# Feed-forward weights of a hybrid encoder block: every low part made by GpSimd, row differences in four parts, down's first activations loaded earlier

## The chip, the cores and the metric

The kernel runs on 1 core of one Trainium2 chip. The metric is the device time of one execution in microseconds (us), given as the median of several runs. A profiled execution is one more run, with a trace of every instruction on the engines: PE (matrix products; PEld is its weight load), DVE (VectorE), ACT (ScalarE), POOL (GpSimd) and SP (SyncE, which here only issues DMAs). Each engine works through its own queue in the order in which the program was laid out, and a waiting instruction holds up all that stands behind it.

## The reference, cut to what matters

All data is float32: x is 1024 rows of 1024, and the change touches only the last part of the layer, the gated feed-forward network of width 2816.

```
hs = hs + mixer_block(rmsnorm(hs, norm_mix), ...)
h  = rmsnorm(hs, norm_ffn)
hs = hs + (silu(h @ w_gate) * (h @ w_up)) @ w_down      # 1024 -> 2816 -> 1024
out = rmsnorm(hs, norm_final)[meta rows dropped]
```

## The kernel before, in words

**Precision.** A float32 product is made of three products of a shorter type (`F32R`): each operand x is cast on ACT to its high part h (`wh`, `yah`, `oph`), and another engine subtracts, l = x - h (`wl`, `yal`, `opl`). I call the first the cast and the second the rest. Every product then runs hh, hl and lh into one PSUM tile.

**Stages.** The mixer ends with `o0` to `o3` (line 1152) at about 1551 us. Then follows the network: 22 keys `wg0`, `wu0`, ... `wg10`, `wu10`, each 256 columns of the gate or up weights, and after them 11 keys `wd0` to `wd10` of the down weights. `gate_up_plain` (line 1169) runs `wg0` and `wu0` as plain products: 8 products of 24 matmuls, in the order half 0 of the rows (two of `wg0`, two of `wu0`), then half 1. The other 20 keys go through `wino` (line 1195): a Strassen-Winograd scheme in which the 2 x 2 blocks of the weights (A11, A12, A21, A22) and of the rows (B11 to B22) are combined, so that seven products of 12 matmuls replace eight. Their order is A11, A12, S2, S3, S1, A22, S4. I call one such key a block.

**Weights.** `next_w` (line 188) keeps one key loaded ahead of the one in use. `load_wino` (line 147) loads a key in two halves on SP (line 157; I call them the first and the second half; A11 and A21 lie in the first, A12 and A22 in the second). POOL makes the sums in place: S1 = A21 + A22 (line 179), A21 = A11 - A21, which is S3 (line 180), A11 = S1 - A11, which is S2 (line 181), and A12 = A12 - A11, which is S4 (line 184). Each of the seven matrices is split in `split_q` (cast line 172, rest line 173). The rests of A11, A12, S2 and S3 go to DVE, those of S1, A22 and S4 to POOL. Two tiles limit the overlap: the raw halves have two buffers (`wraw`), so the first half of the next key waits until S3 and the S4 sum of this key are made, and its second half until the rest of S4 is made; S3, A22 and S4 have three tiles in all (`yah`, `yal`), so they wait for products 4, 6 and 7 of the key before.

**Evacuation.** Six PSUM tiles rotate under the products (`pc`; the names mm, yo, ss, cb, yo, yd). Product 1 is copied out by ACT (line 1214), the others are added up on DVE (`plus`, line 1210, tile `mu`). A gate key's four results go through Silu on ACT (line 1232), an up key's are multiplied on DVE (line 1164, tile `fsg`) and stored by SP (line 1165, `d_act`).

**Rows.** `norm2_second(k)` (line 1110) makes, for one k of 4, the second half of the rows and their differences T1, T2, T3: eight transposes on PE (line 1092, tile `tp`, two buffers), casts on ACT, and seven DVE and three POOL operations (lines 1096 to 1130). All four parts are traced right behind the first of the eight plain products. Behind them the pool of `hs` closes, and the pool `fa` (the tiles fsg, mu, s1, yah, yal) opens in its place, which is what `fa_box` says.

**Down.** `load_act(s)` (line 1236) reads four activation tiles back (line 1244) and splits them (cast line 1245, rest line 1246 on DVE and POOL in turn). `load_act(0)` is traced behind the last block, then eight loads of `hs` (line 1255); `down` (line 1257) runs 16 products of 6 matmuls (line 1266) a key and adds each into `hs` on DVE (line 1268).

**What sets the order.** The code is traced in program order; a planner (the scheduler of the kernel framework) then lays out each engine's queue before the run. It goes by what it reckons to be ready, by its own durations, and takes what was traced earlier among what is ready. So a queue can hold an operation of the next key ahead of one of this key, and on the chip that order is fixed.

Of the kernel before, what the change touches and what calls it, by code (L numbers as in the profile page):

```python
# [8 lines left out]
F32 = mybir.dt.float32  # L9
F32R = mybir.dt.float32r  # L10
AF = mybir.ActivationFunctionType
ALU = mybir.AluOpType
# [3 lines left out]
P = 128  # L16
# [14 lines left out]
NFF = FF // P  # L31
# [26 lines left out]
def tile_hybrid_block(  # L58
# [7 lines left out]
    V, S, GP, PE, SP = nc.vector, nc.scalar, nc.gpsimd, nc.tensor, nc.sync  # L66
    x = x[0]
    out = out[0]
# [55 lines left out]
    plan = []  # L124
    ready = []

    def load_w(view, lo):

        a, b = view.shape[1], view.shape[2]
        wh = wts.tile([P, 2048], F32R, name="wh", tag="wh")  # L130
        wl = wts.tile([P, 2048], F32R, name="wl", tag="wl")
        h3 = wh[:, : a * b].rearrange("p (a b) -> p a b", b=b)
        l3 = wl[:, : a * b].rearrange("p (a b) -> p a b", b=b)
        st = a // 2
        for i in range(2):
            raw = wts.tile([P, 1024], F32, name="wraw", tag="wraw", bufs=2)
            r3 = raw[:, : st * b].rearrange("p (a b) -> p a b", b=b)
            SP.dma_start(out=r3, in_=view[:, i * st:(i + 1) * st, :])
            sl = slice(i * st, (i + 1) * st)
            S.copy(out=h3[:, sl], in_=r3)  # L140
            (V if lo[i] == "v" else GP).tensor_tensor(out=l3[:, sl], in0=r3, in1=h3[:, sl].bitcast(F32), op=ALU.subtract)  # L141
        return h3, l3
# [3 lines left out]
    def load_wino(view):  # L146

        fa = fa_box[0]
        raws = []
        for i in range(2):
            raw = wts.tile([P, 1024], F32, name="wraw", tag="wraw", bufs=2)
            r3 = raw.rearrange("p (a b) -> p a b", b=256)
            SP.dma_start(out=r3, in_=view[:, 4 * i:4 * i + 4, :])
            raws.append(r3)
        a11, a21, a12, a22 = (raws[h][:, :, j * P:(j + 1) * P] for h in range(2) for j in range(2))
        wh = wts.tile([P, 2048], F32R, name="wh", tag="wh")  # L160
        wl = wts.tile([P, 2048], F32R, name="wl", tag="wl")
        slots = [tuple(t[:, 512 * i:512 * i + 512] for t in (wh, wl)) for i in range(4)]
        k4 = lambda t: t.rearrange("p (a b) -> p a b", b=P)
        res = {}

        def split_q(name, src, eng):
            if name in ("S3", "A22", "S4"):
                pair = tuple(fa.tile([P, 512], F32R, name=n_, bufs=3) for n_ in ("yah", "yal"))
            else:
                pair = slots.pop(0)  # L170
            h, l = (k4(t) for t in pair)
            S.copy(out=h, in_=src)  # L172
            eng.tensor_tensor(out=l, in0=src, in1=h.bitcast(F32), op=ALU.subtract)  # L173
            res[name] = h, l

        s1 = k4(fa.tile([P, 512], F32, name="s1", bufs=1))
        split_q("A11", a11, V)
        split_q("A12", a12, V)
        GP.tensor_tensor(out=s1, in0=a21, in1=a22, op=ALU.add)
        GP.tensor_tensor(out=a21, in0=a11, in1=a21, op=ALU.subtract)  # L180
        GP.tensor_tensor(out=a11, in0=s1, in1=a11, op=ALU.subtract)
        split_q("S2", a11, V)
        split_q("S1", s1, GP)
        GP.tensor_tensor(out=a12, in0=a12, in1=a11, op=ALU.subtract)  # L184
        split_q("S3", a21, V)
        split_q("A22", a22, GP)
        split_q("S4", a12, GP)
        return res

    def next_w(key):  # L190

        while plan and len(ready) < 2:
            k, view, lo = plan.pop(0)
            ready.append((k, load_wino(view) if lo is None else load_w(view, lo)))
        k, w = ready.pop(0)
        assert k == key, (k, key)
        return w
# [328 lines left out]
    sgs = []  # L526
# [124 lines left out]
    def op_tile():  # L651
        h = opp_box[0].tile([P, 512], F32R, name="oph", tag="oph")
        l = opp_box[0].tile([P, 512], F32R, name="opl", tag="opl")
        return h, l
# [323 lines left out]
    def halves(hh):  # L978
        return slice(hh * 512, hh * 512 + 512)
# [131 lines left out]
    def norm2_second(k):  # L1111

        ps = norm2_cols(1, k)
        b12 = B["B12", k] = split_cols(ps, k, x_pair("x", 4))
        h11, l11 = (t.bitcast(F32) for t in B["B11", k])
        t1 = fx.tile([P, 512], F32, name="t1", bufs=2)
        V.scalar_tensor_tensor(out=t1, in0=ps, scalar=prm(R_NF, k), in1=h11, op0=ALU.mult, op1=ALU.subtract)
        V.tensor_tensor(out=t1, in0=t1, in1=l11, op=ALU.subtract)
        B["T1", k] = split_t(op_tile(), t1, GP)
        ps = norm2_cols(1, k + 4)  # L1120
        B["B22", k] = split_cols(ps, k + 4, op_tile())
        if k % 2 == 0:
            t2f[0] = fx.tile([P, D], F32, name="t2", bufs=2)
        t2 = t2f[k + 1] = t2f[0][:, 512 * (k % 2):512 * (k % 2) + 512]
        V.scalar_tensor_tensor(out=t2, in0=ps, scalar=prm(R_NF, k + 4), in1=t1, op0=ALU.mult, op1=ALU.subtract)
        B["T2", k] = split_t(x_pair("y", 8), t2, GP)
        t3 = fx.tile([P, 512], F32, name="t3", bufs=2)
        V.scalar_tensor_tensor(out=t3, in0=ps, scalar=prm(R_NF, k + 4), in1=b12[0].bitcast(F32), op0=ALU.mult,
                               op1=ALU.subtract)
        V.tensor_tensor(out=t3, in0=t3, in1=b12[1].bitcast(F32), op=ALU.subtract)  # L1130
        B["T3", k] = split_t(x_pair("y", 8), t3, GP)
# [31 lines left out]
    def act_out(s, j, hh, ps_or_sum, sg):  # L1163
        V.tensor_tensor(out=sg, in0=ps_or_sum, in1=sg, op=ALU.mult)
        SP.dma_start(out=d_act[2 * s + j, :, halves(hh)], in_=sg)
# [2 lines left out]

    def gate_up_plain(s):

        ws, sgs = [next_w(f"wg{s}")], {}
        for hh in range(2):
            for u_ in range(2):
                if u_ == len(ws):
                    ws.append(next_w(f"wu{s}"))
                wh, wl = ws[u_]
                for j in range(2):
                    js = slice(j * P, (j + 1) * P)
                    ps = pc()
                    o = [B[(("B11", "B21"), ("B12", "B22"))[hh][k // 4], k % 4] for k in range(KC)]  # L1180
                    mm3(ps, [wh[:, k, js] for k in range(KC)], [wl[:, k, js] for k in range(KC)],
                        [t[0] for t in o], [t[1] for t in o])
                    if not fa_box:
                        with tc.issue_after(last_mm[0].ins):
                            for k in range(4):
                                norm2_second(k)
                        hs_ctx.close()
                        fa_box.append(fa_ctx.enter_context(tc.tile_pool(name="fa", bufs=1)))
                    if u_ == 0:
                        sgs[j, hh] = fa_box[0].tile([P, 512], F32, name="fsg", bufs=4)  # L1190
                        S.activation(out=sgs[j, hh], in_=ps, func=AF.Silu)
                    else:
                        act_out(s, j, hh, ps, sgs.pop((j, hh)))

    def wino(key, emit):

# [24 lines left out]
        emit(1, 0, plus(prod("A22", "T4"), u3, u3))  # L1221
        emit(0, 1, plus(prod("S4", "B22"), u, u))

    gate_up_plain(0)
    for k in range(4):
        norm2_last(k)
    for s in range(1, NFF // 2):
        sgs = {}

        def emit_gate(j, hh, r):  # L1230
            sgs[j, hh] = fa_box[0].tile([P, 512], F32, name="fsg", bufs=4)
            S.activation(out=sgs[j, hh], in_=r, func=AF.Silu)

        wino(f"wg{s}", emit_gate)
        wino(f"wu{s}", lambda j, hh, r: act_out(s, j, hh, r, sgs.pop((j, hh))))


    def load_act(s):

        res = {}  # L1240
        for hh in range(2):
            for j in range(2):
                h, l = res[j, hh] = op_tile()
                SP.dma_start(out=l.bitcast(F32), in_=d_act[2 * s + j, :, halves(hh)])
                S.copy(out=h, in_=l.bitcast(F32))
                (V, GP)[j].tensor_tensor(out=l, in0=l.bitcast(F32), in1=h.bitcast(F32), op=ALU.subtract)
        return res

    res = load_act(0)
    fa_ctx.close()  # L1250
    fx_ctx.close()
    ffp = ctx.enter_context(tc.tile_pool(name="ffp", bufs=2))
    hs = [ffp.tile([P, D], F32, name=f"hs{i}", bufs=1) for i in range(NTT)]
    for i in range(NTT):
        SP.dma_start(out=hs[i], in_=d_hs[i])

    def down(s, res, after=None):
        wh, wl = next_w(f"wd{s}")
# [45 lines left out]
                q.dma_start(out=out[i * P:(i + 1) * P, t0:t0 + n], in_=h_)  # L1304

    for s in range(NFF // 2):
        nxt = load_act(s + 1) if s + 1 < NFF // 2 else None
        down(s, res, None if nxt else final_norm)
        res = nxt

# [28 lines left out]
```

## Time and profile before

| | us |
|---|---|
| median of 3 runs (2266.1 to 2270.68) | 2270.66 |
| profiled execution, its own time | 2271.47 |
| its span, first to last instruction | 2269.8 |
| busy in the span: PE / DVE / POOL / ACT | 2174.4 / 1525.8 / 1060.0 / 824.8 |
| mean granted TensorE clock | 0.995 of full speed |

A row of the timeline is: start, duration, engine, line, operation, out<-in, count, and in square brackets the time that the engine stood idle before it and what ended that. Busy times of PE include the modelled ends of pipelined matmuls, so two neighbours overlap; the spacing of starts is the safer measure.

### The profile page before, as it was taken

The numbers are of one execution on the slowest core, as the hardware profiler recorded it, in microseconds if no ns is written. First come the engines' busy times: TensorE is split into PE (matmuls) and PEld (weight loads), VectorE is DVE, ScalarE is ACT, GpSimd is POOL, SyncE is SP. The second block draws the span as 40 slices with busy tenths as digits, with TensorE's granted clock in tenths as the row PEclk, the third lists the DMA queues.
The fourth block names the chain that finished last, engine by engine and source line by source line (L and its number), as shares of the span: only waits on it lengthen the run. The fifth ranks groups of instructions, "written<-read, shape, count | busy, mean of one in ns | idle before, by whom it ended". The sixth has DMA issues, their size and how long they took to land.

```text
span 2269.8 us, 31785 instructions
## 1 busy us (share of the span) xinstructions
PE 2174.4 (96%) x11863; PEld 1854.1 (82%) x11863; DVE 1525.8 (67%) x1932; ACT 824.8 (36%) x1522; POOL 1060.0 (47%) x887
## 2 busy tenths in 40 slices
PE   7999999999999999988899999998999999989998
PEld 7999999999998766665676778897888777768886
DVE  4389898997881487877897665527544544467666
ACT  6333342323232355444555554214322222231212
POOL 3383755822112486867787331015554445443212
PEclk9999999999999999999999999999999999999999
DMA  4222222233236575756763742412222222263211
GB/s 141 80 67 83 75 75 75 75 119 106 85 110 201 179 220 164 213 156 202 228 184 113 264 149 94 143 60 92 72 75 75 81 77 70 89 250 102 95 64 75
DMA packets 238147, 276.83 MB, mean 122 GB/s; under 512 B 20776, under 2 KB 176024, under 8 KB 237992
## 3 DMA queue, kind: packets, MB, share of 16 engines
q1 hardware_dynamic: 225176, 253.35, 35.8%
q10 hardware_dynamic: 12816, 21.44, 2.6%
q8 instruction: 94, 1.54, 0.3%
q14 instruction: 61, 0.50, 0.1%
HBM read 189.96 MB, written 84.77 MB: 121 GB/s over the span
## 4 chain that ended last, share of the span: by engine, by line
PE 30%; POOL 7%; issue 7%; DMA 5%; DVE 3%; ACT 2%; SPq 0%; POOLq 0%; DVEq 0%; ACTq 0%
PE yo L243 5%; PE mm L243 4%; PE yo L1266 3%; PE ss L243 3%; PE yd L243 2%; PE cb L243 2%; PE mm L1266 2%; PE yd L1266 2%; PE cb L1266 2%; PE ss L1266 2%; POOL yal L173 1%; DMA wraw<-d_vn 1%; POOL wraw L180 1%; PE yo L1152 1%; POOL wraw L184 1%
## 5 line engine op out<-in xcount | busy, mean ns | idle before, releaser
L141 POOL TENSOR_TENSOR wl<-wraw,wh 128x1024 fp32r<-128x1024 f32 (+1 forms) x83 | 201.9, 2443 | 545.9 <-ACT wh L140 523.1
L243 PE MATMUL mm<-hnh,wh 128*128 128x352 f32 (+4 forms) x1208 | 410.8, 340 | 16.2 <-ACT w L600 14.8
L243 PE MATMUL mm<-hnh,wl 128*128 128x352 f32 (+4 forms) x1208 | 403.6, 334 | 4.3 <-POOL wl L141 4.3
L243 PE MATMUL mm<-hnl,wh 128*128 128x352 f32 (+4 forms) x1208 | 405.8, 336 | 0.4 <-DVE hnl L425 0.4
L243 PEld LDWEIGHTS mm<-hnh,wh 128*128 128x128 f32 x1208 | 228.1, 189 | 31.0 <-ACT w L600 18.8
L521 DVE SCALAR_TENSOR_TENSOR acc<-ap,pr,acc 128x1024 f32<-128x1024 f32 x192 | 247.5, 1289 | 6.3
L243 PEld LDWEIGHTS mm<-hnh,wl 128*128 128x128 f32 x1208 | 228.1, 189 | 14.6 <-POOL wl L141 4.9
L243 PEld LDWEIGHTS mm<-hnl,wh 128*128 128x128 f32 x1208 | 228.1, 189 | 9.8 <-issue 1.2
L140 ACT CAST wh<-wraw 128x1024 fp32r<-128x1024 f32 (+1 forms) x132 | 134.4, 1042 | 239.3 <-PE mm L243 54.1
L173 DVE TENSOR_TENSOR wl<-wraw,wh 128x512 fp32r<-128x512 f32 x60 | 60.8, 1014 | 194.3 <-ACT wh L172 194.3
L521 DVE SCALAR_TENSOR_TENSOR acc<-xp,pr,acc 128x1040 f32<-128x1040 f32 x120 | 156.7, 1306 | 4.0
L319 PE MATMUL mm<-wh,hnh 128*128 128x256 f32 x512 | 144.0, 282 | 5.1 <-ACT w L322 5.1
L319 PE MATMUL mm<-wl,hnh 128*128 128x256 f32 x512 | 144.0, 282 | 0.0
L319 PE MATMUL mm<-wh,hnl 128*128 128x256 f32 x512 | 143.8, 281 | 0.0
L805 POOL TENSOR_SCALAR_AFFINE_SELECT sel<-adh 128x512 fp32r<-128x512 f32 x128 | 98.0, 786 | 71.0 <-ACT wh L140 41.6
L172 ACT CAST wh<-wraw 128x512 fp32r<-128x512 f32 x60 | 37.2, 621 | 224.9 <-DMA wraw<-in_w_up_dram 114.6
L141 DVE TENSOR_TENSOR wl<-wraw,wh 128x1024 fp32r<-128x1024 f32 x49 | 91.6, 1872 | 37.6 <-ACT wh L140 32.0
L560 POOL TENSOR_TENSOR tap<-tap 128x1024 f32<-128x1024 f32 x40 | 96.1, 2402 | 34.4 <-ACT tap L556 33.3
L173 POOL TENSOR_TENSOR yal<-wraw,yah 128x512 fp32r<-128x512 f32 x40 | 55.4, 1395 | 116.4 <-ACT yah L172 110.3
L243 PE MATMUL mm<-oph,wh 128*128 128x512 f32 x224 | 92.1, 411 | 15.1 <-ACT w L703 10.9
L319 PEld LDWEIGHTS mm<-wh,hnh 128*128 128x128 f32 x512 | 96.3, 188 | 5.9 <-ACT w L322 5.8
L805 POOL TENSOR_SCALAR_AFFINE_SELECT sel<-adl 128x512 fp32r<-128x512 f32 x128 | 99.3, 798 | 0.1
(506 smaller groups left out, 5790.4 us busy)
## 6 DMA issues: line engine op xcount, KB each, us to landing
wraw<-in_w_in_dram SPq DMA_DIRECT2D x72, 512.0 KB, 3.9
xc<-d_x SPq DMA_DIRECT2D x64, 256.0 KB, 3.4
wraw<-in_w_gate_dram SPq DMA_DIRECT2D x22, 512.0 KB
wraw<-in_w_up_dram SPq DMA_DIRECT2D x22, 512.0 KB, 3.8
d_act<-fsg SPq DMA_DIRECT2D x44, 256.0 KB, 3.9
wraw<-in_w_down_dram SPq DMA_DIRECT2D x22, 512.0 KB, 4.7
opl<-d_act SPq DMA_DIRECT2D x44, 256.0 KB, 3.6
d_x<-xa ACTq DMA_DIRECT2D x16, 520.0 KB, 2.6
```

The lines of the kernel that those rows point to most:

```text
L140: S.copy(out=h3[:, sl], in_=r3)
L141: (V if lo[i] == "v" else GP).tensor_tensor(out=l3[:, sl], in0=r3, in1=h3[:, sl].bitcast(F32), op=ALU.subtract)
L172: S.copy(out=h, in_=src)
L173: eng.tensor_tensor(out=l, in0=src, in1=h.bitcast(F32), op=ALU.subtract)
L180: GP.tensor_tensor(out=a21, in0=a11, in1=a21, op=ALU.subtract)
L184: GP.tensor_tensor(out=a12, in0=a12, in1=a11, op=ALU.subtract)
L243: tie(PE.matmul(out_, **kw))
L319: PE.matmul(ps[:, :256], lhsT=a[:, sl], rhs=bb[:, k, :], start=(k == 0 and q_ == 0), stop=(k == KC - 1 and q_ == 2))
L521: V.scalar_tensor_tensor(out=out_ if last else acc, in0=sl(k), scalar=w(k), in1=acc, op0=ALU.mult, op1=ALU.add)
L560: GP.tensor_tensor(out=t, in0=t, in1=part, op=ALU.add)
L805: GP.affine_select(out=dst, in_=hbc(src, self.c, h0, 4, P, P), pattern=[[0, 4], [-1 if back else 1, P]], compare_op=ALU.is_ge, fill=0.0, b ...
L1266: PE.matmul(ps, lhsT=a[:, sl], rhs=bb[:, k, t0:t0 + n], start=(k == 0 and q_ == 0), stop=(k == 1 and q_ == 2))
```

## The change

1. `split_q` loses its engine argument: the rests of A11, A12, S2 and S3 go to POOL as well. All seven rests of a key, besides its four sums, are then POOL's.
2. In `gate_up_plain` one part of `norm2_second` is traced behind each of the first four products. Their results stay in PSUM (`held`); after the fourth the pool `fa` opens, the four are put out (`put`), and the load of `wg1` is traced there (`preload`) and no longer behind the first product.
3. `load_act(0)` is traced inside the last block, behind the first result of `wu10` (product 2), and `load_act(1)` between the fourth and the fifth load of `hs`.

```diff
-        def split_q(name, src, eng):
+        def split_q(name, src):
...
             S.copy(out=h, in_=src)
-            eng.tensor_tensor(out=l, in0=src, in1=h.bitcast(F32), op=ALU.subtract)
+            GP.tensor_tensor(out=l, in0=src, in1=h.bitcast(F32), op=ALU.subtract)
             res[name] = h, l
...
-        split_q("A11", a11, V)
-        split_q("A12", a12, V)
+        split_q("A11", a11)
+        split_q("A12", a12)
...
-        split_q("S2", a11, V)
-        split_q("S1", s1, GP)
+        split_q("S2", a11)
+        split_q("S1", s1)
         GP.tensor_tensor(out=a12, in0=a12, in1=a11, op=ALU.subtract)
-        split_q("S3", a21, V)
-        split_q("A22", a22, GP)
-        split_q("S4", a12, GP)
+        split_q("S3", a21)
+        split_q("A22", a22)
+        split_q("S4", a12)
         return res
 
-    def next_w(key):
-
-        while plan and len(ready) < 2:
+    def preload(ahead=1):
+        while plan and len(ready) < ahead + 1:
             k, view, lo = plan.pop(0)
             ready.append((k, load_wino(view) if lo is None else load_w(view, lo)))
+
+    def next_w(key):
+
+        preload(0 if plan and plan[0][0] == "wg1" and not fa_box else 1)
...
+        def put(u_, j, hh, ps):
+            if u_ == 0:
+                sgs[j, hh] = fa_box[0].tile([P, 512], F32, name="fsg", bufs=4)
+                S.activation(out=sgs[j, hh], in_=ps, func=AF.Silu)
+            else:
+                act_out(s, j, hh, ps, sgs.pop((j, hh)))
...
-                    if not fa_box:
-                        with tc.issue_after(last_mm[0].ins):
-                            for k in range(4):
-                                norm2_second(k)
+                    if fa_box:
+                        put(u_, j, hh, ps)
+                        continue
+                    held.append((u_, j, hh, ps))
+                    with tc.issue_after(last_mm[0].ins):
+                        norm2_second(2 * u_ + j)
+                    if len(held) == 4:
                         hs_ctx.close()
                         fa_box.append(fa_ctx.enter_context(tc.tile_pool(name="fa", bufs=1)))
...
+                        for h_ in held:
+                            put(*h_)
+                        preload()
...
+        def emit_up(j, hh, r):
+            act_out(s, j, hh, r, sgs.pop((j, hh)))
+            if s == NFF // 2 - 1 and (j, hh) == (0, 0):
+                acts.append(load_act(0))
...
-    res = load_act(0)
+    res = acts.pop()
...
     for i in range(NTT):
         SP.dma_start(out=hs[i], in_=d_hs[i])
+        if i == 3:
+            acts.append(load_act(1))
...
-        nxt = load_act(s + 1) if s + 1 < NFF // 2 else None
+        nxt = acts.pop() if acts else load_act(s + 1) if s + 1 < NFF // 2 else None
```

## Rows read from the trace of the kernel before

**Rows 1.** The page, part 1: busy us (share of the span) and instructions.

```profile
PE 2174.4 (96%) x11863; PEld 1854.1 (82%) x11863; DVE 1525.8 (67%) x1932; ACT 824.8 (36%) x1522; POOL 1060.0 (47%) x887
```

**Rows 2.** Busy time by stretch: length; PE, PEld, DVE, ACT, POOL; PEclk, DMA share, GB/s.

```profile
1551.00:1606.00 55.00, 49.57 (x229) 39.09 (x228) 42.98 (x49) 25.75 (x42) 37.93 (x26) 1.00 0.16 51
1606.00:1800.00 194.00, 194.00 (x841) 157.34 (x840) 91.14 (x120) 55.25 (x96) 93.74 (x66) 1.00 0.25 76
1800.00:2006.00 206.00, 196.76 (x842) 156.61 (x840) 97.95 (x130) 58.68 (x102) 101.39 (x70) 1.00 0.27 85
2006.00:2028.00 22.00, 14.60 (x58) 10.29 (x58) 18.00 (x23) 7.38 (x11) 10.09 (x6) 1.00 0.85 296
```

**Rows 3.** Timeline of PE: first matmuls of products, from 1606 to 2007 us.

```profile
1606.27 0.39 PE L243 MATMUL mm<-oph,wh 128*128 128x512 f32 x1
...
1625.67 0.39 PE L243 MATMUL yo<-oph,wh 128*128 128x512 f32 x1
...
1899.95 0.39 PE L243 MATMUL ss<-oph,yah 128*128 128x512 f32 x1
...
1906.79 0.47 PE L243 MATMUL yo<-oph,wh 128*128 128x512 f32 x1 [1.07 <-DVE mu L1210]
...
2006.89 0.48 PE L1266 MATMUL ss<-wh,oph 128*128 128x512 f32 x1 [0.80 <-DVE mu L1210]
```

**Rows 4.** Timeline of DVE in one block.

```profile
1904.92 1.11 DVE L173 TENSOR_TENSOR wl<-wraw,wh 128x512 fp32r<-128x512 f32 x1 [2.60 <-ACT wh L172]
1905.96 0.68 DVE L1210 TENSOR_TENSOR mu<-yo,mu 128x512 f32<-128x512 f32 x1
...
1907.35 0.68 DVE L173 TENSOR_TENSOR yal<-wraw,yah 128x512 fp32r<-128x512 f32 x1
```

**Rows 5.** Timeline of POOL in the same block, all its operations.

```profile
1899.89 1.29 POOL L179 TENSOR_TENSOR s<-wraw 128x512 f32<-128x512 f32 x1 [4.43 <-DMA wraw<-in_w_up_dram]
1901.26 1.62 POOL L180 TENSOR_TENSOR wraw<-wraw 128x512 f32<-128x512 f32 x1
1902.95 1.28 POOL L181 TENSOR_TENSOR wraw<-s,wraw 128x512 f32<-128x512 f32 x1
1904.20 1.29 POOL L173 TENSOR_TENSOR wl<-s,wh 128x512 fp32r<-128x512 f32 x1
1905.45 1.72 POOL L184 TENSOR_TENSOR wraw<-wraw 128x512 f32<-128x512 f32 x1
1913.07 1.30 POOL L173 TENSOR_TENSOR yal<-wraw,yah 128x512 fp32r<-128x512 f32 x1 [5.91 <-ACT yah L172]
1915.05 1.29 POOL L173 TENSOR_TENSOR yal<-wraw,yah 128x512 fp32r<-128x512 f32 x1 [0.68 <-ACT yah L172]
```

**Rows 6.** Timeline of ACT in the same block: three casts.

```profile
1911.85 0.62 ACT L172 CAST wh<-wraw 128x512 fp32r<-128x512 f32 x1 [2.55 <-DMA wraw<-in_w_gate_dram]
1912.38 0.62 ACT L172 CAST yah<-wraw 128x512 fp32r<-128x512 f32 x1
...
1914.37 0.60 ACT L172 CAST yah<-wraw 128x512 fp32r<-128x512 f32 x1
```

**Rows 7.** The sum for S4 (line 184): first and last start of the 20, and the second.

```profile
L184 POOL TENSOR_TENSOR wraw<-wraw x20: 1712/1730/1761, 1599.5 to 1987.9; 128x512 f32<-128x512 f32 x20
...
1613.63 1.76 POOL L184 TENSOR_TENSOR wraw<-wraw 128x512 f32<-128x512 f32 x1
```

**Rows 8.** POOL groups, 1613 to 1995 us: busy us, mean ns; idle before and its releasers.

```profile
L179 POOL TENSOR_TENSOR s<-wraw 128x512 f32<-128x512 f32 x18 | 23.2, 1291 | 74.0 <-DMA wraw<-in_w_up_dram 39.4 <-DMA wraw<-in_w_gate_dram 34.6
```

**Rows 9.** Timeline of SP in the same block: two issues.

```profile
1895.49 0.38 SPq L157 DMA_DIRECT2D wraw<-in_w_up_dram  x1
1896.04 0.38 SPq L1165 DMA_DIRECT2D d_act<-fsg  x1
```

**Rows 10.** Longest waits of PE, first 1551 to 1606 us, then 2006 to 2028 us.

```profile
PE tp L1092 <- DVE t L1128: 2.8, 1, 2.8
...
PE mm L1266 <- DVE mu L1210: 2.4, 1, 2.4
```

More of the change, by code (lines that the diff above doesn't have):

```diff
@@ L1169, in gate_up_plain @@
     def gate_up_plain(s):
-        ws, sgs = [next_w(f"wg{s}")], {}
+        ws, sgs, held = [next_w(f"wg{s}")], {}, []
+        def put(u_, j, hh, ps):
[4 more added lines that the diff above has]
+                act_out(s, j, hh, ps, sgs.pop((j, hh)))
         for hh in range(2):
@@ L1182, in gate_up_plain @@
                         [t[0] for t in o], [t[1] for t in o])
-                    if not fa_box:
-                        with tc.issue_after(last_mm[0].ins):
-                            for k in range(4):
-                                norm2_second(k)
+                    if fa_box:
[5 more added lines that the diff above has]
+                    if len(held) == 4:
                         hs_ctx.close()
                         fa_box.append(fa_ctx.enter_context(tc.tile_pool(name="fa", bufs=1)))
[L1189 to L1193, printed above, removed]
+                        for h_ in held:
+                            put(*h_)
+                        preload()
     def wino(key, emit):
@@ L1222, in wino, with load_act @@
         emit(0, 1, plus(prod("S4", "B22"), u, u))
+    def load_act(s):
+        res = {}
+        for hh in range(2):
+            for j in range(2):
+                h, l = res[j, hh] = op_tile()
+                SP.dma_start(out=l.bitcast(F32), in_=d_act[2 * s + j, :, halves(hh)])
+                S.copy(out=h, in_=l.bitcast(F32))
+                (V, GP)[j].tensor_tensor(out=l, in0=l.bitcast(F32), in1=h.bitcast(F32), op=ALU.subtract)
+        return res
+    acts = []
     gate_up_plain(0)
@@ L1234, in tile_hybrid_block @@
         wino(f"wg{s}", emit_gate)
[L1235 to L1247, printed above, removed]
-    res = load_act(0)
+        def emit_up(j, hh, r):
+            act_out(s, j, hh, r, sgs.pop((j, hh)))
+            if s == NFF // 2 - 1 and (j, hh) == (0, 0):
+                acts.append(load_act(0))
+        wino(f"wu{s}", emit_up)
+    res = acts.pop()
     fa_ctx.close()
```

## The prediction

> **What bounds the kernel now.** I read the busy shares first [rows 1]: PE is busy 96% of the span, so only PE's idle time can be won, and whatever makes PE wait more is lost. The busy time by stretch [rows 2] says where that idle time lies in the part the change touches: 5.4 us of 55 while the rows' differences are made, none from 1606 to 1800 us, 9.2 us from 1800 to 2006 us and 7.4 us at the start of down. The reader should see that POOL is not full anywhere here: 101 us of 206.
>
> The middle stretch decides, since it holds 20 equal blocks. Seven product starts apart an undisturbed block takes 1625.67 - 1606.27 = 19.40 us [rows 3]; 20 of them are 388.0 us, and the 20 took 2006.89 - 1606.27 = 400.6, so 12.6 us are lost, all after 1800 us. PE's wait at 1906.79 us is for an addition on DVE [rows 3]. That addition, at 1905.96 [rows 4], empties a PSUM tile of six products before, and stands in DVE's queue behind the rest of S2 of the next key, made only from 1904.92 to 1906.03 [rows 4]. So PE waits for the loading of weights, by way of DVE's queue.
>
> How fast does the loading go? The sum for S4 comes once a block: from 1613.63 to 1987.9 us in 18 intervals [rows 7], 20.8 us each, against PE's 19.4. The loading is the slower of the two; PE lives on its lead until 1800 us and then keeps step with it.
>
> Why 20.8, when POOL works some 10 us of it? One block on POOL [rows 5]: the sums and the rest of S1 run back to back to 1907.2; then POOL idles 5.91 us until the cast of A22, works 2 x 1.3 us, and idles again, 4.43 us in this block and 74.0/18 = 4.1 us on average [rows 8], until the second half of the next key has landed. The first pause is the one to understand. A22's tile was free when product 6 ended, at 1899.95 [rows 3], and its data had been there as long. But ACT made its cast at 1912.38, behind the cast of A11 of the **next** key at 1911.85, which waited for that key's first half [rows 6], loaded only after the rest of S3 (1907.35 + 0.68 [rows 4]). This is the order of a queue and no need of the data. The loading is therefore one closed ring: second half lands, sums and rests, first half of the next key lands, casts, rests of A22 and S4, second half of the next key.
>
> **The four rests go to POOL.** First, does the ring keep its order? The planner lays the queues by its own durations, and one of its orders bounds them. It put the second half's load ahead of the store of the block's last result [rows 9]. The load is ready after a cast and a rest on POOL, the store after an addition and a multiplication on DVE, both counted from product 7's end. So it reckons a rest on POOL at under 2 x 0.68 - 0.6 = 0.8 us, about what DVE takes for one [rows 4], where POOL takes 1.29 [rows 5]. In its plan S3's rest waits for product 4's end in any case, and moving it from DVE to POOL delays the next first half by some 0.1 us; eight POOL operations of under 0.8 us ahead of it still fit before that product ends. I expect A11's cast, and now A11's rest on POOL too, to stay ahead of A22 and S4.
>
> Then every POOL operation of a block lies on the ring, one behind another, and so do both loads:
> - eleven operations (the seven of [rows 5] and four rests) at 1.34 us, which is 1.29 us and 0.05 to the next start: 14.7;
> - the second half's load: 4.1 [rows 8];
> - the first half's load and A11's cast: from S3's rest, 1908.03, to 1911.85 + 0.62 [rows 6]: 4.5.
>
> That is 23.3 us. Two of the seven took 1.62 and 1.72 us, the others 1.28 to 1.30 [rows 5]; S4's sum, the longest, ran its first 0.58 us beside DVE's rest of S2 [rows 4]. With DVE's rests gone I take 1.29 for all and add 0.4 us a block for the multiplications that stay on DVE: 23.7. The lowest the rows allow is 22.4 (eleven at 1.25, the shortest spacing, 1904.20 to 1905.45), the highest 24.9 (eleven at the mean of the seven, 1.40, and the gap, and the 4.43 us load). The Trainium skill, GPSIMD Engine Reference, Key points, says that POOL shares its SBUF interfaces with DVE and is disturbed by DVE instructions with two SBUF inputs. By that alone a block without DVE's rests would have no slowed operation but beside a multiplication, and the sum would be 23.3 to 23.7. The trace agrees only in part: the rest of S1 took 1.29 us although its last half ran beside DVE's rest of S2.
>
> Per block 23.7 - 20.8 = 2.9 us, 18 times: **+52.2**. The first interval is 14.2 now (1599.5 to 1613.63 [rows 7]); with the sum 1.3, a cast and a start 0.7, S4's rest 1.3, the load 4.1 and six operations 8.0 I work out 15.4: +1.2. The first S4 sum stands behind three more rests (A11, A12, S2), less what DVE took for two of them: +3.1. From the last S4 sum to the end of the products 18.2 us pass now (1987.9 to 2006.1), part of it DVE's lag; the ring itself needs the rest of S3, the load, a cast, half of `wd0`'s rest (two rests' worth), A22, S4 and the last product, 14 to 16: -2 (0 to -4). Sum of this part: **+54.5**. Nothing is gained on DVE in return: its queue has no more casts to wait for, but PE then waits for the weights, and for ACT's copies, which stand behind the same casts.
>
> **Rows' differences in four parts.** It removes no work: 32 transposes, DVE's 28 and POOL's 12 operations stay. What it can remove are PE's 5.4 us [rows 2], the longest a 2.8 us wait for a PSUM tile that DVE had not emptied [rows 10]. One part a product gives DVE 5.5 us each time (24 matmuls, 2 x 19.40/7) for about 6.1 us of work (28 of the 49 operations that keep it busy 43 us here [rows 2], by four); the last part falls right before the product that needs it, so I leave 1.4 us of stall: **-4** (0 to -5.4). The first four results wait in four of six PSUM tiles until the pool opens, at least 5 us before a product wants one back: nothing. The load of `wg1` is traced later, but its high and low tiles are those of `wg0`, free only after the sixth product: nothing beyond the +3.1 above.
>
> **Activations earlier.** `load_act(0)` issues four loads, four casts and four rests (two on POOL, behind the rest of S4, two on DVE); SP issues them in the last block, ahead of `wd0`'s halves. `load_act(1)` passes four loads of `hs`. Down's start loses 7.4 us [rows 2], waiting for block results still queued on DVE [rows 10]. DVE will not lag now, but `wd0`'s second half comes late in a ring that is late: **-4** (0 to -7.4).
>
> **Sum.** The profiled execution's 2271.5 + 54.5 - 4 - 4 = **2318**. It lies 0.8 us above the median of the runs, so nothing is taken off for that. A measurement of this kernel can tell about 0.2%, 4.5 us, from no change.
>
> **Rivals.**
> *The other side: the ring opens.* If the planner's reckoning of POOL is long enough to bring A11's cast behind those of A22 and S4, POOL no longer waits for the first half: the ring is 14.7 + 4.1 and at most a cast, 19.4 at the utmost, and PE sets the pace. It decides at one place, the order of casts on ACT, and its point is a ring of 19.4 us. PE then gets the 12.6 us back, with 4 and 6 us from the other parts: 2271.5 - 22.6 = **2249**. For it: the planner need only see one cast later. Against it: the bound of 0.8 us, and that this order stands now although A22 had been free for 12 us. The Trainium skill, Perfetto Trace Analysis, Identifying the Most-Contended Engine, would have the engine of highest occupancy set the time; by that rule POOL at 14.7 of 19.4 us has room and this rival wins. The trace speaks against the rule here: POOL was half busy and its ring set the pace all the same [rows 2].
> *A11's rest only changes place.* If on POOL it comes behind A22's and S4's, it runs while the second half loads: 1.3 us less a block, 18 times, **2295**.
> *Gain and loss cancel.* Should the rests cost the ring under 0.5 us a block, because POOL filled pauses that I count as needed, the parts sum to 2266 to 2275. It needs another order too; little speaks for it.
> That the change doesn't do what it says can be left out for the rests, whose engine is written in the code. For `load_act(0)` it is inside its range.
>
> **How the numbers follow.** The ring kept: 0.62, 2318, own range 2290 to 2342 (22.4 to 24.9 us a block, which is 23 below and 22 above, and a few us of the other terms). A11's rest behind: 0.18, 2295. The ring opens: 0.14, 2249. Cancel: 0.04. Above 2342: 0.02. Slower is 0.62 + 0.18 + 0.02 = 0.82, same 0.04, faster 0.14. From 2274 to 2342 the range holds the first two cases nearly whole; the opened ring is left out.
>
> **What would show it.** Right: S4 sums 23 to 24.5 us apart; on POOL a pause of some 4 us before A11's rest and one before S1's sum, and none else; PE idle some 3 to 4 us in each block from the third or fourth on; DVE idle before its additions, waiting for PE. Wrong: A22's and S4's casts ahead of the next key's A11 on ACT, and block starts 19.4 us apart to the end. For the parts: fewer waits of `tp` on DVE before 1606 us, and PE busy more than 14.6 of the first 22 us of down.

## The result, and the profile after

The changed kernel takes 2329.51 us (median of 4 runs, 2327.74 to 2331.16) against 2270.67 (2266.1 to 2271.01): a ratio of 1.0264, 95% interval 1.0248 to 1.0279, 58.8 us slower. The prediction was 2318, slower, in a range of 2274 to 2342.

The page of the kernel after, part 1, answers to [rows 1]:

```profile
PE 2201.4 (95%) x11863; PEld 1870.0 (80%) x11863; DVE 1462.2 (63%) x1852; ACT 822.9 (35%) x1522; POOL 1137.8 (49%) x967
```

DVE has its 80 rests less and POOL 80 operations more, as the code says. POOL is busy 49% of the span. PE's busy time has grown by 27 us although it runs the same 11863 matmuls; part of that is its clock, told at the end.

Busy time by stretch of the kernel after, against [rows 2] (length; PE, PEld, DVE, ACT, POOL; PEclk, DMA share, GB/s):

```profile
1551.00:1612.00 61.00, 53.29 (x253) 42.88 (x252) 38.90 (x46) 27.48 (x46) 41.73 (x32) 0.97 0.12 39
1612.00:1700.00 88.00, 88.00 (x383) 71.22 (x382) 29.57 (x40) 21.57 (x38) 54.62 (x42) 1.00 0.24 70
1700.00:2068.00 368.00, 324.43 (x1306) 250.56 (x1305) 103.23 (x138) 90.95 (x162) 219.25 (x170) 0.96 0.25 74
2068.00:2090.00 22.00, 16.24 (x50) 11.66 (x49) 17.87 (x22) 6.67 (x10) 9.38 (x6) 0.77 0.89 293
```

PE lives on its lead until 1700 us, a hundred microseconds less than before, and from then on waits in every block. What it waits for is no longer DVE: the longest waits of PE from 1612 to 2068 us (us in total, times, longest) are

```profile
PE yo L246 <- POOL wl L173: 13.5, 8, 1.9
PE ss L246 <- POOL wl L173: 8.6, 6, 1.9
PE cb L246 <- POOL wl L173: 7.4, 5, 1.9
PE mm L246 <- POOL wl L173: 5.2, 4, 1.9
PE yd L246 <- POOL wl L173: 3.8, 2, 1.9
```

The pace of the loading, by the sums for S4 (the group's row, then the second of the 20), against [rows 7]:

```profile
L184 POOL TENSOR_TENSOR wraw<-wraw x20: 1267/1279/1312, 1607.4 to 2047.7; 128x512 f32<-128x512 f32 x20
...
1624.11 1.29 POOL L184 TENSOR_TENSOR wraw<-wraw 128x512 f32<-128x512 f32 x1
```

(2047.7 - 1624.11)/18 = 23.5 us a block; before it was 20.8, and PE needs 19.4. One block on POOL, against [rows 5], with a time in brackets wherever POOL stood idle:

```profile
1900.10 1.29 POOL L179 TENSOR_TENSOR s<-wraw 128x512 f32<-128x512 f32 x1 [4.05 <-DMA wraw<-in_w_up_dram]
1901.46 1.28 POOL L180 TENSOR_TENSOR wraw<-wraw 128x512 f32<-128x512 f32 x1
1902.70 1.28 POOL L173 TENSOR_TENSOR wl<-wraw,wh 128x512 fp32r<-128x512 f32 x1
...
1908.89 1.29 POOL L173 TENSOR_TENSOR yal<-wraw,yah 128x512 fp32r<-128x512 f32 x1
1914.73 1.30 POOL L173 TENSOR_TENSOR wl<-wraw,wh 128x512 fp32r<-128x512 f32 x1 [4.55 <-ACT wh L172]
1915.97 2.55 POOL L173 TENSOR_TENSOR yal<-wraw,yah 128x512 fp32r<-128x512 f32 x2
1922.84 1.29 POOL L179 TENSOR_TENSOR s<-wraw 128x512 f32<-128x512 f32 x1 [4.32 <-DMA wraw<-in_w_gate_dram]
```

Eight operations run back to back from 1900.10, then come a pause of 4.55 us until the cast of the next key's A11, three rests (A11, A22, S4), and a pause of 4.32 us for the second half. ACT in the same block, against [rows 6]:

```profile
1914.03 0.62 ACT L172 CAST wh<-wraw 128x512 fp32r<-128x512 f32 x1 [6.58 <-DMA wraw<-in_w_gate_dram]
1914.56 0.62 ACT L172 CAST yah<-wraw 128x512 fp32r<-128x512 f32 x1
...
1915.61 0.60 ACT L172 CAST yah<-wraw 128x512 fp32r<-128x512 f32 x1
```

The order is kept: the cast of A11 (next key) waits 6.58 us for its DMA, and those of A22 and S4 stand behind it.

Where the time went, from the starts of the first products of each stage: 3.1 us by the first product of `wg0`, in code that both kernels share (that start lies between 1549.6 and 1554.2 us in the profiled executions of this document); 3.5 us while the rows' differences are made (first product of `wg0` to first block 58.7 us, before 55.3); 54.2 us in the 20 blocks (454.8, before 400.6); -1.5 us from the first product of down to the end (261.4, before 262.9). Together 59.2, the difference of the two spans.

### The profile page after: what moved, and what is told of

It reads as the page before. It is cut to its first block, busy times and chain, and to the rows that moved or that the text cites. A ratio compares the mean times of both kernels' runs of the same rounds, so it can differ in the third digit from the quotient of the medians.

```text
span 2329.0 us, 31722 instructions
## 1 busy us (share of the span) xinstructions
PE 2201.4 (95%) x11863; PEld 1870.0 (80%) x11863; DVE 1462.2 (63%) x1852; ACT 822.9 (35%) x1522; POOL 1137.8 (49%) x967
## 3 DMA queue, kind: packets, MB, share of 16 engines
q8 instruction: 94, 1.54, 0.3%
## 4 chain that ended last, share of the span: by engine, by line
PE 28%; POOL 12%; DMA 9%; DVE 2%; issue 2%; ACT 1%; SPq 0%; POOLq 0%; DVEq 0%; ACTq 0%
PE mm L246 5%; PE yo L246 4%; DMA wraw<-in_w_up_dram 3%; PE yo L1287 3%; POOL wl L173 3%; POOL yal L173 3%; DMA wraw<-in_w_gate_dram 3%; PE ss L246 2%; PE yd L246 2%; PE cb L1287 2%; PE ss L1287 2%; PE cb L246 2%; PE mm L1287 2%; PE yd L1287 2%; POOL wraw L180 1%
## 5 line engine op out<-in xcount | busy, mean ns | idle before, releaser
L246 PE MATMUL mm<-hnh,wh 128*128 128x352 f32 (+4 forms) x1208 | 411.6, 341 | 16.0 <-ACT w L603 14.6
L173 POOL TENSOR_TENSOR wl<-wraw,wh 128x512 fp32r<-128x512 f32 x60 | 80.9, 1349 | 87.9 <-ACT wh L172 83.4
L1222 DVE TENSOR_TENSOR mu<-yo,mu 128x512 f32<-128x512 f32 x47 | 31.7, 688 | 109.4 <-ACT mu L1226 67.9
```

What stands on the lines that cost most here:

```text
L173: GP.tensor_tensor(out=l, in0=src, in1=h.bitcast(F32), op=ALU.subtract)
L246: tie(PE.matmul(out_, **kw))
L1222: V.tensor_tensor(out=dst, in0=ps, in1=m, op=ALU.add)
```

## The experiments

The theory (A): the loading is one ring closed by ACT's queue, in which the cast of the next A11 stands ahead of those of A22 and S4. A rest moved to POOL lengthens the ring, by its 1.29 us less what it no longer costs elsewhere on the ring; open the ring and the rests cost nothing. Rivals: (B) POOL is simply too slow for eleven operations a block; (C) in the kernel before, it is DVE's queue as such that holds PE.

The experiments ran on four chips, on which the kernel before took 2267.3 (experiments 1 to 3), 2270.9 (4 to 7), 2269.8 (8 to 11) and 2261.5 us (12); so ratios are compared. The three columns on the right are from one profiled execution each: first product of `wg0` to first block, the 20 blocks, first product of down to the end. "Order" is the edit of experiment 2, "B22" that of experiment 8.

| | edits | us | ratio (95%) | rows | blocks | down |
|---|---|---|---|---|---|---|
| before | | | 1 | 55.3 | 400.6 | 262.9 |
| after | 1, 2, 3 | 2329.5 | 1.0264 (1.0248, 1.0279) | 58.7 | 454.8 | 261.4 |
| 1 | 1 | 2321.7 | 1.0242 (1.0225, 1.0259) | 55.2 | 454.4 | 258.3 |
| 2 | 1, 2, 3, order | 2253.8 | 0.9939 (0.9924, 0.9954) | 59.6 | 388.0 | 253.5 |
| 3 | order | 2247.8 | 0.9918 (0.99, 0.9936) | 55.2 | 388.0 | 254.9 |
| 4 | two rests of 1 | 2299.0 | 1.0127 (1.0112, 1.0143) | 56.4 | 430.3 | 259.5 |
| 5 | 2 | 2274.2 | 1.0017 (1.0009, 1.0026) | 59.7 | 401.5 | 258.7 |
| 6 | 3 | 2269.1 | 0.9997 (0.9986, 1.0008) | 55.2 | 399.4 | 258.7 |
| 7 | 3, order | 2248.5 | 0.9905 (0.9891, 0.9919) | 55.3 | 388.0 | 252.2 |
| 8 | 2, B22 | 2272.5 | 1.0012 (1.0003, 1.0021) | 57.4 | 401.2 | 258.2 |
| 9 | 2, 3, order | 2252.2 | 0.9926 (0.9909, 0.9943) | 58.8 | 388.0 | 255.0 |
| 10 | 3, order, B22 | 2246.5 | 0.9897 (0.9883, 0.9912) | 52.0 | 388.0 | 251.6 |
| 11 | 2, 3, order, B22 | 2252.7 | 0.9920 (0.9906, 0.9934) | 57.4 | 388.0 | 254.6 |
| 12 | 1, 3, order, B22 | 2246.7 | 0.9939 (0.9926, 0.9952) | 52.0 | 388.0 | 252.1 |

**1. Edit 1 alone: the four rests to POOL.**

```diff
-        split_q("A11", a11, V)
-        split_q("A12", a12, V)
+        split_q("A11", a11, GP)
+        split_q("A12", a12, GP)
...
-        split_q("S2", a11, V)
+        split_q("S2", a11, GP)
...
-        split_q("S3", a21, V)
+        split_q("S3", a21, GP)
```

> Only the four rests go to GpSimd; rows' differences and activations as before. If the ring of the loading carries the loss (theory A), the S4 sums stand 23 to 24 us apart as in the changed kernel (23.5) and the time is 2270.7 + 18 x 2.7 + some 3 us for the first block = 2318 to 2326. If the other two edits carry a good part of the loss (rival), it stays under 2305.

Measured 2321.7 us, 54.5 above before, nearly the whole loss; the blocks take as long as with the full change. The first expectation holds and its rival falls. The S4 sums:

```profile
L184 POOL TENSOR_TENSOR wraw<-wraw x20: 1263/1280/1302, 1602.7 to 2041.8; 128x512 f32<-128x512 f32 x20
```

**2 and 3. The order of two casts.** To the kernel after (2) and to the kernel before (3) one thing is added: the cast of A11 is issued behind the previous key's cast of S4. No operation is added, removed or moved to another engine.

```diff
-            S.copy(out=h, in_=src)
+            if name == "A11" and s4_cast:
+                with tc.issue_after(s4_cast[0].ins):
+                    c = S.copy(out=h, in_=src)
+            else:
+                c = S.copy(out=h, in_=src)
+            if name == "S4":
+                s4_cast[:] = [c]
```

> The changed kernel with one order added: the cast of A11 of the next key is queued on ScalarE behind the cast of S4 of this key. All rests stay on GpSimd, nothing else moves. Theory A (one closed ring through the queue order): the ring opens, GpSimd no longer waits for the first half, 4.1 + 10 x 1.3 us stay under the 19.4 us of TensorE, blocks start 19.4 us apart to the end, time 2252 to 2266. Rival B (GpSimd is simply too slow for eleven operations a block, whatever their order): S4 sums stay over 22 us apart and the time over 2300.

> The kernel before with the same order added, rests on VectorE and GpSimd as before. Theory A: its ring of 20.8 us opens too, the 12.6 us lost after 1800 us come back and some of the 7.4 us at the start of down, time 2250 to 2260. Rival C (what holds TensorE after 1800 us is VectorE's queue as such, not the ring): the waits for the mu additions stay and the time is 2267 to 2273.

Measured 2253.8 and 2247.8 us, the second 2 us below the range that theory A gave. In experiment 2 all eleven operations still run on POOL, but the blocks take 388.0 us, 20 x 19.4. Its window from the first block to down, the same of experiment 3, and one block on ACT in experiment 2 (line numbers are shifted by the edit; L177 is the cast, and L175 that of A11):

```profile
1611.13:1999.13 388.00, 388.00 (x1681) 314.69 (x1680) 152.84 (x183) 123.00 (x204) 281.40 (x215) 1.00 0.29 89
```

```profile
1609.46:1997.46 388.00, 388.00 (x1681) 314.71 (x1680) 216.78 (x259) 123.18 (x206) 198.97 (x139) 1.00 0.29 90
```

```profile
1899.36 0.62 ACT L177 CAST yah<-wraw 128x512 fp32r<-128x512 f32 x1 [1.21 <-PE yo L253]
...
1902.17 0.62 ACT L177 CAST yah<-wraw 128x512 fp32r<-128x512 f32 x1 [1.28 <-PE ss L253]
1902.93 0.62 ACT L175 CAST wh<-wraw 128x512 fp32r<-128x512 f32 x1
```

The casts of A22 and S4 now wait for the products that free their tiles, and A11's cast, behind them, waits for nothing. On POOL (L180 is the rest, L186 the sum S1) the long pause for the first half is gone, and A11's rest follows that of S4 at once:

```profile
1902.87 1.29 POOL L180 TENSOR_TENSOR yal<-wraw,yah 128x512 fp32r<-128x512 f32 x1 [1.53 <-ACT yah L177]
1904.12 1.28 POOL L180 TENSOR_TENSOR wl<-wraw,wh 128x512 fp32r<-128x512 f32 x1
1907.89 1.30 POOL L186 TENSOR_TENSOR s<-wraw 128x512 f32<-128x512 f32 x1 [2.49 <-DMA wraw<-in_w_gate_dram]
```

PE is busy for 388.00 of 388.00 us with POOL at 281.4, 73%, which is more than the 60% (273.5 of 454.8 us) at which POOL held it up in the changed kernel. B falls. In experiment 3 DVE keeps its four rests and PE does not wait in the blocks either: C falls; the late rest of [rows 4] was late by the ring. One thing moves with the cast: A11's rest, which needs it, also comes behind the others, on POOL in experiment 2 and on DVE in experiment 3. The runs show what the two are worth together.

**4. Half the dose: A12's and S2's rests to POOL.**

```diff
-        split_q("A12", a12, V)
+        split_q("A12", a12, GP)
...
-        split_q("S2", a11, V)
+        split_q("S2", a11, GP)
```

> The kernel before with two of the four rests moved to GpSimd, A12's and S2's. The closed ring (theory A): two more operations of 1.29 us lie on it, less 0.8 us because L180 and L184 no longer run beside a rest on DVE and up to 0.5 us because S3's rest on DVE no longer waits for S2's; S4 sums 22.1 to 22.7 us apart where they were 20.8 and are 23.5 with all four; 18 x 1.3 to 1.9 = 23 to 34 us and 1 us at the first block: 2291 to 2302. The rival, that only the move of A11's rest counts, because that alone stands in the pause between two keys: S4 sums 20.5 to 21.3 us apart, 2264 to 2276.

Measured 1.0127; the medians lie 28.1 us apart. The S4 sums, first to last and the second:

```profile
L184 POOL TENSOR_TENSOR wraw<-wraw x20: 1275/1287/1312, 1600.4 to 2017.5; 128x512 f32<-128x512 f32 x20
...
1615.84 1.31 POOL L184 TENSOR_TENSOR wraw<-wraw 128x512 f32<-128x512 f32 x1
```

(2017.5 - 1615.84)/18 = 22.3 us, between 20.8 and 23.5. The rival, that only A11's rest counts, falls. But a rest doesn't count with its full 1.29 us: two add 1.5 us to a block and four 2.7, some 0.7 each. Part of the difference is on POOL: S4's sum has gone from a median of 1730 ns [rows 7] to 1287 now that DVE no longer runs the rest of S2 beside it, and the sums for S3 and S2 have become shorter by 0.3 and 0.2 us. Another part is in the pauses: POOL's idle time was 10.7 us a block before, is 10.3 with two rests moved and 9.3 with four; that fits that some of DVE's rests had stood on the ring already.

**5 and 6. Edits 2 and 3 alone**, the kernel before otherwise; cut to the core:

```diff
-                            for k in range(4):
-                                norm2_second(k)
+                    held.append((u_, j, hh, ps))
+                    with tc.issue_after(last_mm[0].ins):
+                        norm2_second(2 * u_ + j)
```

```diff
+            if s == NFF // 2 - 1 and (j, hh) == (0, 0):
+                acts.append(load_act(0))
...
+        if i == 3:
+            acts.append(load_act(1))
```

> The kernel before with edit 2 alone (the rows' differences in four parts). The prediction's step: 4 us gained (0 to 5.4), so 2262 to 2267 where the kernel before takes 2267. The theory formed on the trace after: spread over four products the work still stands behind late casts in ACT's queue, and PE is stopped at the last part; from the first product of wg0 to the first block it takes 58 to 60 us where the kernel before takes 55.3, and the whole takes 1 to 7 us more, 2268 to 2274. Pace of the S4 sums 20.8 us under both.

> The kernel before with edit 3 alone (first activations of down loaded earlier). The prediction's step: 4 us gained (0 to 7.4), 2260 to 2267. The theory formed on the trace after, that the start of down waits for block results and wd0's second half and not for the activations: 0 to 2 us gained, 2265 to 2268. Nothing changes ahead of the last block under either: S4 sums 20.8 us apart.

Edit 2 costs 0.17% (0.09 to 0.26), some 4 us where 4 were to be won. Edit 3 can't be told from nothing. For edit 2 the timeline of PE says where:

```profile
1587.41 0.39 PE L246 MATMUL cb<-xh,wl 128*128 128x512 f32 x1
1591.67 0.80 PE L246 MATMUL ss<-oph,wh 128*128 128x512 f32 x1 [3.87 <-ACT oph L1099]
1592.26 0.63 PE L246 MATMUL cb<-xh,wh 128*128 128x512 f32 x1
1592.69 0.63 PE L246 MATMUL cb<-xl,wh 128*128 128x512 f32 x1
```

PE waits 3.87 us for the cast of B22 of the last part. On ACT that cast (L1099) stands behind the cast for T1 (L1110), which only a block will need:

```profile
1590.41 0.62 ACT L1110 CAST oph<-t 128x512 fp32r<-128x512 f32 x1 [4.05 <-DVE t L1121]
1590.93 0.68 ACT L1099 ACTIVATE oph<-tp,pr 128x512 fp32r<-128x512 f32 x1
```

And T1 is late because on DVE it stands behind an operation for T4 (`norm2_last`, L1141), which needs a result of POOL:

```profile
1586.95 1.76 DVE L1141 TENSOR_TENSOR t<-t,opl 128x512 f32<-128x512 f32 x1 [1.77 <-POOL t L1140]
1588.63 1.74 DVE L1121 TENSOR_TENSOR t<-t,opl 128x512 f32<-128x512 f32 x1
```

Three of the four T4 operations stand so, each right ahead of a part's T1, and DVE waits 0.86, 1.22 and 1.77 us at them.

Neither order is new with edit 2. In the kernel before, T1's last cast (L1107) stands ahead of B22's (L1096) as well, and the T4 operations (L1138) stand among the parts:

```profile
1587.03 0.62 ACT L1107 CAST oph<-t 128x512 fp32r<-128x512 f32 x1 [2.85 <-DVE t L1118]
1587.56 0.68 ACT L1096 ACTIVATE oph<-tp,pr 128x512 fp32r<-128x512 f32 x1
```

```profile
1567.49 1.75 DVE L1138 TENSOR_TENSOR t<-t,opl 128x512 f32<-128x512 f32 x1 [0.52 <-POOL t L1137]
1576.68 1.78 DVE L1138 TENSOR_TENSOR t<-t,opl 128x512 f32<-128x512 f32 x1 [1.19 <-POOL t L1137]
1583.54 1.77 DVE L1138 TENSOR_TENSOR t<-t,opl 128x512 f32<-128x512 f32 x1 [0.53 <-POOL t L1137]
```

What differs is the pace. These operations stand 9.2 and 6.9 us apart before, and 9.0 and 10.0 with edit 2 (1567.93, 1576.91 and 1586.95), so the last cast of B22 starts 39.6 us behind the first product of `wg0` where it started 36.5 behind it.

**7. Edit 3 in the opened ring.** Experiments 3 and 6 together.

> The version with the cast of the next A11 behind the cast of S4, otherwise as before, and edit 3 added. Theory A: in the opened ring the start of down has no stall left, so earlier activations give nothing: 2245 to 2251, within 2.5 us of that version without edit 3 (ratio to before 0.9905 to 0.993). The rival, that the activations' own latency counts as soon as the blocks are quick: 3 to 6 us less, 2241 to 2245 (0.9885 to 0.9903).

0.9905, at the edge of the first expectation; its interval overlaps that of experiment 3 and reaches into the rival's range. The first 22 us of down, against [rows 2], first in experiment 3 (the order alone), then with edit 3 as well:

```profile
1997.46:2019.46 22.00, 22.00 (x96) 17.83 (x95) 15.27 (x21) 2.17 (x5) 2.93 (x2) 1.00 0.93 340
```

```profile
1995.07:2017.07 22.00, 21.08 (x91) 16.67 (x90) 15.40 (x21) 2.90 (x5) 3.05 (x2) 1.00 0.89 315
```

With the order alone PE is busy all the 22 us, where it was 14.60 before: nothing is left at the start of down for edit 3 to win. Down as a whole took 254.9 us in the one trace and 252.2 in the other; kernels whose down is the same differ by as much (258.3 to 262.9 in the column).

**8. Edit 2 with B22 ahead of T1.** Within a part, B22's transposes, cast and rest are traced before the work for T1.

```diff
         b12 = B["B12", k] = split_cols(ps, k, x_pair("x", 4))
+        ps2 = norm2_cols(1, k + 4)
+        B["B22", k] = split_cols(ps2, k + 4, op_tile())
...
         B["T1", k] = split_t(op_tile(), t1, GP)
-        ps = norm2_cols(1, k + 4)
-        B["B22", k] = split_cols(ps, k + 4, op_tile())
```

> The kernel before with edit 2, and within each part the transposes, casts and rests of B22 traced ahead of the work for T1. The theory that the four parts lost by queue order (T1's cast, needed only in the blocks, stood ahead of the cast of B22, for which PE waited 3.87 us): from the first product of wg0 to the first block 55.5 to 57 us instead of the 59.7 of edit 2 alone and the 55.3 of the kernel before; the time 2.5 to 4 us under that of edit 2 alone, a ratio to before of 0.9998 to 1.0008. The rival, that a part's own chain is too long to stand right ahead of the product that needs it, in whatever order: 59 to 60 us again, 1.0015 to 1.002.

57.4 us: neither. The new order takes 2.3 us off the stage. It doesn't explain the 4.4 us that edit 2 adds, for without edit 2 the same order takes off 3.3 (experiments 7 and 10), and what edit 2 adds is then 5.4. DVE now waits 2.5 us at each of three T4 operations,

```profile
1584.52 1.75 DVE L1141 TENSOR_TENSOR t<-t,opl 128x512 f32<-128x512 f32 x1 [2.54 <-POOL t L1140]
```

where experiment 10 has one such wait, and PE's waits for `tp` tiles come between the products (1.54, 1.17 and 1.54 us). Holding T4's operations back was not tried, so whether these waits or a part's own chain of operations cost the time stays open.

**9 to 11. The other edits in the opened ring.** 9 is the change without edit 1, with the order; 10 is experiment 7 with B22 ahead of T1; 11 is 9 with it.

> All of the change but the move of the rests, with the cast of the next A11 behind that of S4. If the terms add up: edit 2 costs its 3 to 4.5 us in the opened ring as well, so 0.9920 to 0.9935 where the version without edit 2 had 0.9905 to 0.9918. The rival, that the opened ring hides the late start because the weights have a lead: no difference, 0.9900 to 0.9915.

> The rests as before, the cast of the next A11 behind that of S4, edit 3, and B22 ahead of T1 in each part, all four parts behind the first product as before. If PE's 2.8 us wait for a tp tile in the kernel before comes from the same order, it goes: 52 to 54 us from the first product to the first block, 0.9890 to 0.9905. The rival, that the tile is then held longer by T2 and T3 and the wait comes again elsewhere: 55 to 57 us, 0.9905 to 0.992.

> The same with the parts behind four products as in the change. If the queue order was all that stood against the four parts: 53 to 56 us from the first product to the first block, 0.9885 to 0.9910. The rival, a part's own chain: 59 to 60 us, 0.9920 to 0.9935.

By the medians, edit 2 costs some 5 us in the opened ring too (9 against 7: 0.9926 and 0.9905; 11 against 10: 0.9920 and 0.9897; the intervals of each pair just overlap, the stages differ by 3.5 and 5.4 us), and B22 ahead of T1 shortens the stage by 3.3 us where all four parts stand behind the first product. Experiment 11 took 57.4 us in the stage, between its two expectations, as experiment 8 did; its ratio lies at the lower edge of the rival's, a part's own chain. Experiment 10, 0.9897 (0.9883 to 0.9912), beats both kernels of this case.

**12. All four rests on POOL in that version.** Experiment 10 with edit 1.

> All four rests on GpSimd, the cast of the next A11 behind that of S4, B22 ahead of T1 in each part, edit 3, and all four parts behind the first product as before (edit 2 left out). Theory A: with the ring open the place of the rests no longer matters, since eleven operations of 1.3 us and the load stay under the 19.4 us of a block: S4 sums 19.4 us apart, no stall of TensorE in the blocks, within 3 us of the same version with the rests as before (0.9897): 0.988 to 0.991. The rival, that GpSimd at 14.5 of 19.4 us delays the weights at times: stalls on rests from GpSimd in the blocks, 0.992 to 0.996.

By the trace theory A holds: blocks of 388.0 us, no wait of PE in them, S4 sums (1966.1 - 1599.6)/19 = 19.3 us apart, a span of 2244.5 us beside the 2243.0 of experiment 10:

```profile
1604.36:1992.36 388.00, 388.00 (x1682) 314.68 (x1681) 150.34 (x185) 122.20 (x205) 281.50 (x215) 1.00 0.28 90
```

By the ratio the rival's range was hit, 0.9939; but on that chip the kernel before took 2261.5 us, 6 to 9 us less than on the others, while this one took what experiment 10 took elsewhere. Why that chip favours the kernel before is open, and so is a difference of some microseconds between the two places of the rests.

## Why the prediction was right

**The ring (+52.2 predicted).** Right in mechanism, and near in size. The 18 intervals took 23.5 us where 23.7 were worked out: +49.3. The two pauses of a block, by POOL's groups from 1623 to 2048 us (busy us, mean ns, idle before and its releasers), against [rows 8]:

```profile
L173 POOL TENSOR_TENSOR wl<-wraw,wh 128x512 fp32r<-128x512 f32 x54 | 73.2, 1355 | 87.5 <-ACT wh L172 83.0 <-PE mm L246 4.5
...
L179 POOL TENSOR_TENSOR s<-wraw 128x512 f32<-128x512 f32 x18 | 23.2, 1290 | 78.8 <-DMA wraw<-in_w_up_dram 41.2 <-DMA wraw<-in_w_gate_dram 37.7
```

87.5/18 = 4.9 us for the first half and the cast (4.5 taken), 78.8/18 = 4.4 for the second half (4.1 taken). That is 0.7 us more than the sum had, and the eleven operations took 0.9 us less: 23.5 - 9.3 = 14.2 us, where 14.7 and 0.4 were reckoned. The sum counted 0.05 us from one operation's end to the next start, but back to back they start 1.24 us apart, less than one lasts (1901.46 and 1902.70 above). So the nearness of 23.5 to 23.7 is in part luck. So is that of the part's sum: edit 1 alone cost 54.5 us, what it said (+54.5), with the 18 intervals 2.9 us under and the terms below 2.6 us over.

The order on which all this hung was kept, and experiment 2 shows what it was worth: 1.0264 against 0.9939, some 74 us. A11's rest stayed ahead of those of A22 and S4 as well (POOL, 1914.73), so the rival in which it only changes place fell. The reason given for the order, that the planner reckons a rest on POOL at under 0.8 us, is not shown by any run. Its bound took 0.68 us for the multiplication on DVE, which lasts 1.06 in the trace of the kernel before (at 1894.94 us); with that it would be 1.1.

**Its small terms.** The first S4 sum came 1.4 us later than the sixth product's end explains (3.1 predicted), the first interval is 2.5 us longer (1.2), and from the last S4 sum to down 1.0 us more passes (-2). None is larger than 3 us.

**Rows in four parts (-4 predicted).** Wrong in sign: +3.5 in the changed kernel, +4.4 in the stage alone (experiment 5). The step that failed is "one part a product gives DVE 5.5 us each time for about 6.1 us of work": it counted the work and not the waits and the order. Alone, a part takes DVE 9.0 to 10.0 us (experiment 5): T4's operations, 1.8 us each and no part of that sum, stand between the parts, DVE waits for POOL at them, and it waits 1.27 us for B22's cast behind that of T1. The last part then falls right before the product that needs it, and PE waits 3.87 us where 1.4 were left. How the loss divides among these is open: the two orders stood in the kernel before too, and experiments 8 and 11 remove only one of them. The sign that was named, fewer waits for `tp`, hardly came: PE's waits for these tiles in the stage are 3.8 us in the kernel after and were 4.3.

**Activations earlier (-4 predicted).** Not seen: 0.9997 alone (0.9986 to 1.0008). "DVE will not lag now" failed. PE's waits at down's start in the kernel after are for the same additions as before:

```profile
2071.59 0.51 PE L1287 MATMUL cb<-wh,oph 128*128 128x512 f32 x1 [2.37 <-DVE mu L1222]
2081.44 0.50 PE L1287 MATMUL yo<-wh,oph 128*128 128x512 f32 x1 [2.40 <-DVE mu L1222]
```

The late ring makes the last block's results late, whoever makes the rests. What removes these waits is the order (experiments 3 and 7). The sign that was named, PE busy more than 14.6 of the first 22 us of down, came true (16.24) and misleads: 50 matmuls ran in that time where 58 ran before, at a granted clock of 0.77.

**The size of the whole.** The profiled execution took 2330.7 us, 12.7 over the forecast: 7.5 in the rows (+3.5 for -4), 2.5 in down (-1.5 for -4) and the 3.1 ahead of the first product of `wg0`, which no term foresaw; the blocks were foreseen to 0.3 us.

**The rivals.** "The ring opens" was priced at 2249 with 10 us from the other two edits, which they don't give; with the order forced, it is 2253.8. The Trainium skill, Perfetto Trace Analysis, Identifying the Most-Contended Engine, names the engine with the highest occupancy as the one to work on first. In the blocks of the changed kernel that is PE, 411.2 of 454.8 us. POOL's share alone told nothing there: 60% busy it held PE up, 73% busy it did not, and between the two lies the order of one cast and its rest. DVE's gain of 80 rests bought nothing, as forecast: its additions wait for PE and for ACT's copies (16.3 us at 1917 us in the changed kernel).

**The waits foreseen.** "PE idle some 3 to 4 us in each block" was too much: over the 20 blocks PE's idle time is 454.8 - 411.2 = 43.6 us, 2.2 a block. The waits set in later than foreseen, after 1700 us, in the fifth block and not the third or fourth. The rest of the loss does not show as idle; see the last section.

## What to carry to other kernels

Where a stage runs slower than its busiest engine, follow one buffer round: load, cast, rest, last use, next load; if the way leads through an in-order queue in which the next round's work stands ahead of this one's, the pace is the sum of everything on that way. An operation moved from one engine to another then costs what it adds there less what it had cost on the way before: here some 0.7 us a rest of 1.29. And the order of two instructions is worth more than the choice of engine: here one cast moved back gave 0.8% to the kernel before and 3.2% to the changed one. When work is spread out to make room, see in each queue what will then stand between its pieces.

## What the runs showed that was not expected

TensorE's clock fell in stages where it waited, and stayed low for a while after the wait. In experiment 5, by stretch:

```profile
1551.29:1586.00 34.71, 30.89 (x151) 24.63 (x150) 24.32 (x31) 15.50 (x25) 20.33 (x15) 1.00 0.14 46
1586.00:1591.00 5.00, 1.80 (x8) 1.12 (x6) 4.05 (x4) 0.95 (x3) 3.83 (x3) 0.94 0.00 0
1591.00:1597.00 6.00, 5.33 (x13) 4.17 (x14) 5.16 (x6) 3.47 (x7) 5.50 (x4) 0.50 0.24 90
1597.00:1611.00 14.00, 14.00 (x61) 11.36 (x60) 8.04 (x9) 5.83 (x11) 7.55 (x6) 0.99 0.21 52
```

After the wait of 3.87 us the granted clock is 0.50, the lower of its two levels (1.2 GHz), and the matmuls start 0.43 us apart instead of 0.23, until 1596.95. Twelve of them took 5.28 us instead of 2.8: the wait cost 2.5 us more than its own length. The Trainium skill, Advanced Engine Details and Errata, Clock Domains, says in a note that the array's clock is gated to 1.2 GHz when idle; the trace agrees, with 0.50 behind a wait of 3.87 us.

In the blocks of the changed kernel the granted clock is 0.97 on average, and the matmuls show 411.2 us of busy time where experiment 2 shows 388.0 for as many. The clock is worth some 14 of these 23 us (3% of 454.8); where the others come from is open. The ring's sum explains the pace of these blocks without it; but idle time has turned into slow busy time, so a busy share of PE of 90% in that stretch looks better than it is.
